# Multiplying a norm's factor into the products instead of their inputs, in a two-layer decoder step

## The chip, the core and the metric

The kernel runs on one core of a Trainium2 chip. Its time is the device time of one execution in microseconds (us); three runs of the kernel before took 3342.1, 3348.75 and 3351.01. PE is the matrix engine (TensorE), DVE the vector engine, ACT the scalar engine, POOL GpSimd; SP (SyncE) only issues transfers here, and ACT issues those of the weights.

## The reference

Two layers of a decoder process a prompt of 1024 tokens and 64 tokens of 8 sampled sequences, 1088 columns of 1024 features. Each layer is a mixer and a feed-forward, both behind a norm:

```python
def rmsnorm(x, g):
    return x * rsqrt(mean(x * x) + eps) * g

x = x + mixer(rmsnorm(x, norm_mix)) @ w_out
h = rmsnorm(x, norm_ffn)
x = x + (silu(h @ w_gate) * (h @ w_up)) @ w_down
```

The first layer's mixer is a short convolution on a product of two projections beside a linear recurrence (RWKV-7) over 8 heads. The second layer's is causal attention with forget gates over 8 heads, for the samples over 1024 cached rows each in paged memory as well, beside a state-space scan (SSD) in chunks of 128 tokens with its own causal convolution. The states, keys and values are outputs too. A last norm makes y.

## The kernel before

**Tiles.** Activations lie with features on the partitions, 8 tiles of 128 features by the columns of a half. There are two halves: H0 has the 64 sample columns and 512 of the prompt (576, handled in groups of 320 and 256), H1 the other 512. In layer 1's feed-forward the samples go with the second half instead: F0 has 512 columns and F1 576. A weight tile is 128 columns of a product for all 1024 inputs.

**Dense products.** Weights and activations are both split into a high and a low part, and each of the 8 feature tiles takes three matmuls (hh by wh, hl by wh, hh by wl; mm3, lines 204 to 206), all into one of four PSUM banks ("acc"). load_w (line 191) fetches a weight tile on ACT's queue, ACT rounds it to wh (line 196), and POOL, or DVE late in the kernel, takes the difference wl (line 198).

**The norms.** rms (line 227) squares eight tiles on ACT, adds them on DVE (line 239), sums over partitions with matmuls against ones on PE (line 245), takes the power on POOL (line 224) and broadcasts the factor over the partitions with matmuls (line 255). rms_split then makes x * g * r on DVE (line 269) and its two parts (lines 218, 219). These parts are what the next products read, so the next product begins after all of this. A call of rms_split makes 10 yields.

**The order of the work.** The functions are generators, and each yield ends a step. `weave(dense, side, rate)` emits the steps of a dense generator and, for each, `rate` steps of a side generator that does a mixer's small work. There are five weaves, with RATE = (5.5, 6, 1.8, 1.8, 1): the first two put the recurrences of H0 and H1 beside projections and H0's feed-forward; the third and fourth put `side`, which is latency(H0) and then latency(H1), beside third() (H1's layer-0 output and feed-forward, norm, and layer-1 projections) and beside F0's output product and feed-forward (ffn). These two are called with rest=False, and what is then left of the side comes from drain(side) (line 1570). latency(H0) has 32 steps of attention units, 25 of gates by token and scan, and 249 of the cached rows' attention (decode); latency(H1) has 32 attention units and 24 of the scan. F1's feed-forward comes last; its y (line 852) is read back from the buffers where attention and scan of H1 and the samples' decode leave it.

A scheduler orders each engine's instructions at build time by program order and a simulated readiness; the engines then run their queues in order, and wait on semaphores.

**The second half's attention** (line 1111) goes through 4 pairs of heads. For each pair the queries and keys (qa, qb, ka, kb, one buffer each) are loaded by SP. A unit is 128 queries of a head: scores into two PSUM banks ("fs", lines 1153 to 1155), mask and maximum on DVE (lines 1157 to 1161), exponentials on ACT (line 1164), reciprocal and scaling on DVE (lines 1167, 1168), transposes (line 1174), copies (line 1175), products with v (line 1182). The scan (line 1349) comes after it and writes y through ysp1.

Of the kernel before, what the change touches and what calls it, by code (L numbers as in the profile page):

```python
# [19 lines left out]
P = 128  # L20
D = 1024
# [21 lines left out]
CF = (3, 6)  # L43
# [27 lines left out]
# the second feed-forward takes the samples with the second half, since their attention is the last to be done  # L71
# [3 lines left out]
# columns of the parameter pack  # L75
# [9 lines left out]
# columns of the constant packs: 0 for both layers, 1 for the first mixer, 2 for the second, 3 for the cached rows  # L85
# [69 lines left out]
class K:  # L155
    """What the stages share: the builder, the pools and the constants on chip."""

    xp = None
    # PSUM banks: the dense products', the mixers' short-lived ones, their chains', and the ones with sums over many steps
# [26 lines left out]
    def parts(self, H):  # L186
        """Tiles for the two float32r parts of an activation of a half."""
        return [[self.bp.tile([P, H.W], F32R, name=n, tag="%s%d" % (n, H.i), bufs=KT) for _ in range(KT)] for n in ("hh", "hl")]


def load_w(k, src, n=D):
    nc = k.nc
    raw = k.wp.tile([P, D], F32, name="wraw", tag="wraw", bufs=2)[:, :n]
    nc.scalar.dma_start(raw, src)
# [27 lines left out]
def rsqrt(k, out, x):  # L222
    """x ** -0.5 of a few columns."""
# [3 lines left out]
def rms(k, H, xs, width, groups=None, ft=None, tag="acc"):  # L227
    """1 / sqrt(mean over features of x^2 + eps) on every partition: (columns, PSUM bank) per group."""
# [32 lines left out]
def rms_split(k, H, xs, gname):  # L261
    """rmsnorm(x) * g as two float32r parts."""
    nc = k.nc
    h = k.parts(H)
    rs = yield from rms(k, H, xs, D)
    for i in range(KT):
        v = k.ft(H)
        for a, b, r in rs:
            nc.vector.scalar_tensor_tensor(v[:, a:b], xs[i][:, a:b], k.col(gname, i), r, op0=ALU.mult, op1=ALU.mult)
        split(k, h[0][i], h[1][i], v, nc.gpsimd if i % 2 else nc.vector)  # L270
        if i % 2:
            yield
    return h
# [7 lines left out]
class Even:  # L281
    def __init__(self, k, pool):
# [9 lines left out]
        nc.gpsimd.memset(self.o_shift, 0.0)  # L292
        k.load_con(pool, 1)
        # the parts of the two small products' weights: the first part twice, for the two parts of what they take
# [12 lines left out]
        self.dv = pool.tile([P, 30], F32, name="dv")  # L307
        dv = self.dv
        nc.vector.tensor_scalar(dv[:, 0:14], k.pp[:, PP["mu"]:PP["mu"] + 14], -1.0, 1.0, op0=ALU.mult, op1=ALU.add)
        for o, n, f in ((14, "w0", 0.5), (18, "a0", 0.5), (22, "ka", 0.5), (26, "kk", -0.5)):  # L310
            nc.vector.tensor_scalar(dv[:, o:o + 4], k.pp[:, PP[n]:PP[n] + 4], f, None, op0=ALU.mult)
# [22 lines left out]
    def short_conv(self, H, h):  # L334
        k = self.k
        nc = k.nc
        for i in range(4):
# [4 lines left out]
            for a, b in H.groups:  # L342
                nc.scalar.copy(gcs[:, a:b], gemm_tile(k, wc, h, a, b))
# [23 lines left out]
            for a, b in H.groups:  # L367
                pb = gemm_tile(k, wb, h, a, b)
                nc.vector.tensor_mul(cv[:, a:b], cv[:, a:b], pb)
# [3 lines left out]
    def shift_mix(self, H, h, i, dp, ds):  # L373
        """Column tile i of the projection, mixed with the token before: z + mu * (before - z); dp prompt, ds samples."""
# [3 lines left out]
        w = load_w(k, k.A["wi0"][12 + i])  # L378
# [5 lines left out]
        for a, b in H.groups:  # L384
            acc = gemm_tile(k, w, h, a, b)
# [14 lines left out]
    def project(self, H, h):  # L400
# [1300 lines left out]
```

## Time and profile before

| what | value |
|---|---|
| runs | 3342.1, 3348.75, 3351.01 us; median 3348.75 |
| span of the profiled execution | 3342.5 us |
| PE busy | 3166.9 us, 95% |
| DVE busy | 1918.7 us, 57% |
| ACT busy | 1063.7 us, 32% |
| POOL busy | 843.0 us, 25% |

The profiled execution has the span as its own time; nothing else of it is shown, and the span lies between the lowest run and the median. PE is nearly always busy in the records. A busy PE is not PE at its peak: matmuls overlap, their ends are modelled, and a lower granted clock stretches them. So a stretch of the program is read with three numbers: its length, PE's busy time in it and the granted clock, 1.00 being the upper of its two levels.

### The profile page before, as it was taken

How to read it: one execution, taken by the hardware profiler on the slowest of the kernel's cores; microseconds unless marked ns; L12 is line 12 of the kernel's file. 1: busy time of each engine (PE TensorE's matmuls, PEld its weight loads, DVE VectorE, ACT ScalarE, POOL GpSimd, SP SyncE). 2: the span in 40 equal slices, each digit the busy share in tenths (PEclk: the TensorE clock that was granted, in tenths of full speed). 3: DMA queues.
4: the chain of work that ended last, by engine and by line, in shares of the span. 5: the costliest groups of instructions: out<-in, count | busy, mean ns of one | idle time of the engine just before them, and what ended most of it. 6: DMA issues, size and time to landing. Idle time of an engine off the chain costs nothing. (4 is left out here: it accounts for less than half of the span.)

```text
span 3342.5 us, 63321 instructions
## 1 busy us (share of the span) xinstructions
PE 3166.9 (95%) x25213; PEld 2667.2 (80%) x25213; DVE 1918.7 (57%) x3663; ACT 1063.7 (32%) x2083; POOL 843.0 (25%) x565
## 2 busy tenths in 40 slices
PE   7999999999999998999899999999999988999998
PEld 7887667777899998976677676766777767899998
DVE  6766646575544447656665457555646665554445
ACT  4333323333222223345322224232225543322222
POOL 3433233333233333301300102011010002333332
PEclk9999999999999998999899999999999999999999
DMA  5322233221122235543345557875553324232222
GB/s 178 116 66 82 87 99 114 65 65 57 51 72 83 82 112 160 178 151 124 98 155 171 192 161 228 240 233 158 164 177 118 123 89 151 69 104 82 83 82 79
DMA packets 238471, 409.20 MB, mean 122 GB/s; under 512 B 37632, under 2 KB 129664, under 8 KB 238176
## 3 DMA queue, kind: packets, MB, share of 16 engines
q10 hardware_dynamic: 63232, 218.80, 20.2%
q1 hardware_dynamic: 165584, 152.27, 15.2%
q0 software_dynamic: 9360, 34.08, 2.9%
q8 instruction: 199, 3.26, 0.4%
q14 instruction: 96, 0.79, 0.1%
HBM read 352.23 MB, written 52.81 MB: 121 GB/s over the span
## 5 line engine op out<-in xcount | busy, mean ns | idle before, releaser
L204 PE MATMUL acc<-hh,wh 128*128 128x320 f32 (+2 forms) x3720 | 1262.6, 341 | 14.0 <-ACT hh L218 10.7
L206 PE MATMUL acc<-hh,wl 128*128 128x320 f32 (+2 forms) x3720 | 1254.6, 337 | 7.2 <-POOL wl L198 6.4
L205 PE MATMUL acc<-hl,wh 128*128 128x320 f32 (+2 forms) x3720 | 1254.2, 338 | 7.1 <-DVE hl L219 5.1
L198 POOL TENSOR_TENSOR wl<-wraw,wh 128x1024 fp32r<-128x1024 f32 x229 | 549.2, 2399 | 988.3 <-ACT wh L196 931.2
L204 PEld LDWEIGHTS acc<-hh,wh 128*128 128x128 f32 x3720 | 711.2, 192 | 90.6 <-ACT hh L218 14.5
L196 ACT CAST wh<-wraw 128x1024 fp32r<-128x1024 f32 (+1 forms) x398 | 415.9, 1045 | 1145.5 <-PE acc L205 1021.9
L205 PEld LDWEIGHTS acc<-hl,wh 128*128 128x128 f32 x3720 | 712.3, 192 | 71.7 <-DVE hl L219 8.4
L206 PEld LDWEIGHTS acc<-hh,wl 128*128 128x128 f32 x3720 | 712.5, 192 | 70.9 <-POOL wl L198 8.1
L893 DVE TENSOR_TENSOR x<-x,acc 128x320 f32<-128x320 f32 (+2 forms) x528 | 270.6, 528 | 144.8 <-PE acc L206 143.0
L204 PE MATMUL acc<-hidh,wh 128*128 128x320 f32 (+2 forms) x1056 | 349.8, 337 | 3.7 <-ACT hidh L218 3.3
L205 PE MATMUL acc<-hidl,wh 128*128 128x320 f32 (+2 forms) x1056 | 353.2, 335 | 0.0
L206 PE MATMUL acc<-hidh,wl 128*128 128x320 f32 (+2 forms) x1056 | 350.2, 333 | 0.4 <-DVE wl L198 0.4
L198 DVE TENSOR_TENSOR wl<-wraw,wh 128x1024 fp32r<-128x1024 f32 x169 | 205.5, 1217 | 116.5 <-ACT wh L196 96.1
L1297 POOL DMA_INDIRECT kv<-in_cv,vidx x64 | 75.1, 1173 | 630.4 <-DMA kv<-in_ck 363.8
L204 PEld LDWEIGHTS acc<-hidh,wh 128*128 128x128 f32 x1056 | 198.8, 189 | 28.0 <-ACT hidh L218 6.0
L205 PEld LDWEIGHTS acc<-hidl,wh 128*128 128x128 f32 x1056 | 200.1, 190 | 17.5 <-issue 1.4
L206 PEld LDWEIGHTS acc<-hidh,wl 128*128 128x128 f32 x1056 | 200.3, 190 | 16.2 <-issue 0.9
L219 DVE TENSOR_TENSOR hidl<-ft,hidh 128x512 fp32r<-128x512 f32 (+2 forms) x148 | 178.6, 1207 | 57.1 <-ACT hidh L218 55.8
L881 DVE SCALAR_TENSOR_TENSOR ft<-ft,acc 128x320 f32<-128x320 f32 (+2 forms) x132 | 70.1, 531 | 221.4 <-PE acc L206 218.0
L875 DVE SCALAR_TENSOR_TENSOR ft<-ft,acc 128x320 f32<-128x320 f32 (+2 forms) x132 | 69.7, 528 | 190.2 <-ACT ft L874 190.1
L218 ACT CAST hidh<-ft 128x512 fp32r<-128x512 f32 (+2 forms) x148 | 75.1, 507 | 120.4 <-DVE ft L881 117.2
L1249 DVE STREAM_TRANSPOSE kt<-kv 128x1024 f32<-128x1024 f32 x64 | 79.3, 1240 | 35.8 <-DMA kv<-in_ck 21.1
(340 smaller groups left out, 3360.1 us busy)
## 6 DMA issues: line engine op xcount, KB each, us to landing
wraw<-in_wi ACTq DMA_DIRECT2D x100, 512.0 KB
wraw<-in_wg ACTq DMA_DIRECT2D x88, 512.0 KB
wraw<-in_wu ACTq DMA_DIRECT2D x88, 512.0 KB
wraw<-in_wd ACTq DMA_DIRECT2D x88, 512.0 KB
kv<-in_ck SPq DMA_DIRECT2D x512, 64.0 KB
wraw<-in_wo ACTq DMA_DIRECT2D x32, 512.0 KB
ka<-kp SPq DMA_DIRECT2D x48, 128.0 KB
x<-in_xT SPq DMA_DIRECT2D x16, 288.0 KB
```

What stands on the lines that cost most here:

```text
L196: nc.scalar.copy(wh, raw)
L198: k.low.tensor_sub(wl, raw, wh)
L204: mm(acc, wh, xh, start=first, stop=False)
L205: mm(acc, wh, xl, start=False, stop=False)
L206: mm(acc, wl, xh, start=False, stop=last)
L218: k.nc.scalar.copy(hh, v)
L219: (eng or k.nc.vector).tensor_sub(hl, v, hh)
L875: nc.vector.scalar_tensor_tensor(s[:, a:b], s[:, a:b], 1.0, pc, op0=ALU.add, op1=ALU.mult)
L881: nc.vector.scalar_tensor_tensor(s[:, a:b], s[:, a:b], 0.5, pu, op0=ALU.mult, op1=ALU.mult)
L893: nc.vector.tensor_add(xs[n][:, a:b], xs[n][:, a:b], acc[:, :b - a])
L1249: V.transpose(kt, kr)
L1297: nc.gpsimd.indirect_dma_start(out=v, out_offset=None, in_=A["cv"].rearrange("o (s r) c -> (o s) (r c)", r=2), in_offset=bass.IndirectOffs ...
```

## The change

A class Norm takes the place of rms_split. The parts that the products read are made of x * g, without the factor. The sum of squares is kept as the tiles of x are made or arrive. The ones-products, the power, and the broadcast are emitted inside the first product that uses the parts, after its sixth and sixteenth feature tile (third and eighth for a half in one group). The factor, r, goes to SBUF, and each product is multiplied by it on DVE as it leaves PSUM. In the feed-forward the gate's product is multiplied by r for the tanh, and by r again, which covers the factor of the product with w_up.

The first weight tile and the next are fetched before x. In the first layer the recurrence's constants are loaded after three products, H1's norm comes right after, and the second half's short convolution goes ahead of H0's output product instead of beside norms. The weaves keep their rates; the norm's yields are gone. The scan writes its G in L and a decayed state in place; zp has one buffer; the ten first steps of F1, not twenty, stand beside the last of F0's.

```diff
+class Norm:
...
+        self.due = (6, 16) if len(H.groups) > 1 else (3, 8)
...
+    def square(self, x):
+        k = self.k
+        if self.ss is None:
+            self.ss = k.bp.tile([P, self.H.W], F32, name="rn", tag="rn%d" % self.H.i, bufs=1)
+            k.nc.scalar.activation(self.ss, x, AF.Square)
+            return
+        sq = k.ft(self.H)
+        k.nc.scalar.activation(sq, x, AF.Square)
+        k.nc.vector.tensor_add(self.ss, self.ss, sq)
+
+    def part(self, i, x):
+        if not i:
+            self.hl = self.k.parts(self.H)
+        k, g = self.k, self.k.col(self.gname, i)
+        k.nc.scalar.mul(self.hl[0][i], x, g)
+        k.nc.vector.scalar_tensor_tensor(self.hl[1][i], x, g, self.hl[0][i], op0=ALU.mult, op1=ALU.subtract)
+
+    def step(self):
...
+        if self.seen == self.due[0]:
+            pt = k.bank()
+            for j, (l, _, _) in enumerate(H.blocks):
+                nc.tensor.matmul(pt[:, j:j + 1], self.ss[:, l:l + P], k.con("ones"), start=True, stop=True)
+            self.rs = k.bp.tile([P, 16], F32, name="rs", tag="rs", bufs=2)
+            nc.vector.tensor_scalar(self.rs[:, 8:8 + nb], pt[:, :nb], 1.0 / D, EPS, op0=ALU.mult, op1=ALU.add)
+            rsqrt(k, self.rs[:, 0:nb], self.rs[:, 8:8 + nb])
+        elif self.seen == self.due[1]:
...
+                    nc.tensor.transpose(pb[:, c - o:c - o + P], self.rs[:, j:j + 1].to_broadcast([P, P]), k.con("ident"))
...
+                nc.scalar.copy(r[:, o:e], pb[:, 0:e - o])
+            self.r = r
...
@@ gemm_tile
+        if isinstance(h, Norm):
+            h.step()
...
@@ out_ffn
         xs.append(x)
-        yield
-    h = yield from beside(rms_split(k, H, xs, "nf%d" % l), fill)
+        nr.square(x)
+        if n < KT - 1:
+            yield
+    w = load_w(k, A["wg%d" % l][0])
+    for i, x in enumerate(xs):
+        nr.part(i, x)
+    yield
...
             s = k.ft(H)
+            t = k.ft(H)
             for (a, b), pc in zip(H.groups, pg):
-                nc.scalar.activation(s[:, a:b], pc, AF.Tanh, scale=0.5)
-                nc.vector.scalar_tensor_tensor(s[:, a:b], s[:, a:b], 1.0, pc, op0=ALU.add, op1=ALU.mult)
+                nc.vector.tensor_mul(t[:, a:b], pc, nr.r[:, a:b])
+                nc.scalar.activation(s[:, a:b], t[:, a:b], AF.Tanh, scale=0.5)
+            nc.vector.tensor_mul(t, t, nr.r)
+            nc.vector.scalar_tensor_tensor(s, s, 1.0, t, op0=ALU.add, op1=ALU.mult)
...
@@ Odd.dense
-                    nc.scalar.mul(t[:, a:b], gemm_tile(k, w, h, a, b), f)
+                    nc.vector.scalar_tensor_tensor(t[:, a:b], gemm_tile(k, w, h, a, b), f, h.r[:, a:b], op0=ALU.mult, op1=ALU.mult)
...
@@ ssd
-                    g_ = tl([P, 128], "G", 3)
-                    V.scalar_tensor_tensor(g_[:n, :n], L[:n, :n], tok[:n, c, 64 + hd:65 + hd], gt[:n, c, g, :n], op0=ALU.mult, op1=ALU.mult)
+                    V.scalar_tensor_tensor(L[:n, :n], L[:n, :n], tok[:n, c, 64 + hd:65 + hd], gt[:n, c, g, :n], op0=ALU.mult, op1=ALU.mult)
...
@@ hybrid_step
-        x0 = x_in(H0)
         k.pp = cp.tile([P, NPP], F32, name="pp")
         nc.sync.dma_start(k.pp, A["pp"])
+        w0 = load_w(k, A["wi0"][24])
         k.load_con(cp, 0)
+        k.ahead = [fetch(k, A["wi0"][16])]
+        h0 = norm_in(H0)
...
             def third():
-                x1 = yield from ffn0(H1)
-                h = yield from rms_split(k, H1, x1, "nm1")
+                h = yield from ffn0(H1)
                 yield from m.dense(H1, h)
...
-            weave(ffn, islice(ffn1, 20), RATE[4])
+            weave(ffn, islice(ffn1, 10), RATE[4])
```

PE in the second half's attention, in the kernel before: scores (L1155), transposes (L1174) and products with v (L1182) of two units, between them F0's dense matmuls (L204 to 206; hidh and hidl are the parts of the feed-forward's hidden tile).

```order
L206 MATMUL acc<-hh,wl 128x512
L204 MATMUL acc<-hidh,wh 128x512
L205 MATMUL acc<-hidl,wh 128x512
L206 MATMUL acc<-hidh,wl 128x512
L204 MATMUL acc<-hidh,wh 128x512
L1182 MATMUL rk<-pT,vt 64x128 x10
L1155 MATMUL fs<-ka,qa 128x512
L1155 MATMUL fs<-kb,qb 128x512
L1155 MATMUL fs<-ka,qa 128x256
L1155 MATMUL fs<-kb,qb 128x256
L204 MATMUL acc<-hidh,wh 128x512
L1174 MATMUL rk<-con_222,s 128x128 x6
```

The same attention in the changed kernel, where scores are L1233, transposes L1252 and products with v L1260.

```order
L1233 MATMUL fs<-ka,qa 128x512
L1233 MATMUL fs<-kb,qb 128x512
L1233 MATMUL fs<-ka,qa 128x384
L1233 MATMUL fs<-kb,qb 128x384
L1252 MATMUL rk<-con_212,s 128x128 x7
L1233 MATMUL fs<-ka,qa 128x512
L1233 MATMUL fs<-kb,qb 128x512
L1233 MATMUL fs<-ka,qa 128x512
L1233 MATMUL fs<-kb,qb 128x512
L1252 MATMUL rk<-con_212,s 128x128 x7
L1233 MATMUL fs<-ka,qa 128x512
L1233 MATMUL fs<-kb,qb 128x512
```

The dense matmuls that stood between the units stand ahead of them now. In the whole queue, 28 of the 32 units and the scan of H1 come after F0's last dense matmul, with 48 dense matmuls of F1's beside them.

PE at the norm of F1's feed-forward, in the kernel before: the ones-products (L245) and the broadcast (L255) between the last of w_out's products and the first of w_gate's (128x320).

```order
L205 MATMUL acc<-hl,wh 128x256
L206 MATMUL acc<-hh,wl 128x256
L245 MATMUL acc<-con_222,ft 128x1 x5
L255 MATMUL acc<-con_222,rs 128x64
L255 MATMUL acc<-con_222,rs 128x128 x4
L204 MATMUL acc<-hh,wh 128x320
L204 MATMUL acc<-hh,wh 128x256
L205 MATMUL acc<-hl,wh 128x320
```

There in the changed kernel, inside the first product of w_gate: L210 to 212 are mm3, L310 the ones-products, and the transposes that broadcast the factor come some 25 matmuls later.

```order
L212 MATMUL acc<-hh,wl 128x256
L210 MATMUL acc<-hh,wh 128x256
L310 MATMUL rk<-con_212,rn 128x1 x5
L211 MATMUL acc<-hl,wh 128x256
L212 MATMUL acc<-hh,wl 128x256
L210 MATMUL acc<-hh,wh 128x256
```

No dense matmul stands behind the broadcast any more, but for the emptying of its bank.

## Rows read from the trace of the kernel before

**Rows 1.** The page's part 1: busy us, share of the span, instructions of each engine.

```profile
PE 3166.9 (95%) x25213; PEld 2667.2 (80%) x25213; DVE 1918.7 (57%) x3663; ACT 1063.7 (32%) x2083; POOL 843.0 (25%) x565
```

**Rows 2.** Windows round five norms: from:to length, busy (instructions) per engine, clock, DMA.

```profile
640.00:700.00 60.00, 55.57 (x655) 41.36 (x652) 41.33 (x94) 19.40 (x44) 22.03 (x18) 0.91 0.19 60
1250.00:1272.00 22.00, 15.75 (x86) 12.94 (x85) 17.66 (x34) 7.51 (x11) 12.12 (x10) 0.77 0.37 121
1506.00:1520.00 14.00, 10.16 (x49) 8.40 (x45) 9.10 (x20) 5.66 (x14) 3.93 (x3) 0.66 0.31 96
2274.00:2292.00 18.00, 13.77 (x80) 8.22 (x79) 8.09 (x14) 3.17 (x6) 5.97 (x5) 0.62 0.58 167
2883.00:2903.00 20.00, 12.68 (x61) 11.35 (x61) 12.47 (x23) 6.69 (x10) 7.77 (x5) 0.66 0.10 34
```

**Rows 3.** PE's waits, 2883 to 2903: total, times, longest, in us.

```profile
PE acc L245 <- DVE ft L239: 4.1, 1, 4.1
```

**Rows 4.** Windows, the woven stretch at the end of layer 1's mixer.

```profile
2500.00:2700.00 200.00, 199.77 (x1257) 159.52 (x1258) 130.05 (x296) 103.50 (x248) 0.00 (x0) 1.00 0.36 113
2700.00:2812.00 112.00, 98.23 (x498) 75.61 (x497) 64.95 (x142) 40.10 (x84) 18.80 (x12) 0.91 0.36 118
2812.00:2840.00 28.00, 23.06 (x115) 19.54 (x115) 14.80 (x20) 10.21 (x14) 7.37 (x5) 0.94 0.64 205
```

**Rows 5.** Timeline of the start: start, length in us, engine, line, tiles [idle before].

```profile
5.30 0.68 ACT L237 ACTIVATE ft<-x 128x576 f32<-128x576 f32 x1 [2.35 <-DMA x<-in_xT]
...
18.49 2.29 PE L245 MATMUL acc<-con,ft 128*128 128x1 f32 x10 [18.49 <-DVE ft L239]
...
26.13 0.85 PE L204 MATMUL acc<-hh,wh 128*128 128x320 f32 x2 [1.34 <-ACT hh L218]
```

**Rows 6.** Timeline, two units of the second half's attention, 2571 to 2581.

```profile
2571.05 0.50 PE L1155 MATMUL fs<-ka,qa 128*128 128x512 f32 x1
...
2573.97 0.69 ACT L1164 ACTIVATE s<-fs,nm 128x512 f32<-128x512 f32 x1 [0.29 <-DVE nm L1161]
...
2575.17 0.39 PE L1155 MATMUL fs<-ka,qa 128*128 128x512 f32 x1
...
2575.81 0.19 PEld L204 LDWEIGHTS acc<-hidh,wh 128*128 128x128 f32 x1
...
2577.42 0.77 PEld L1174 LDWEIGHTS rk<-con,s 128*128 128x128 f32 x6
...
2578.88 1.53 PE L1182 MATMUL rk<-pT,vt 128*64 128x128 f32 x24
...
2580.34 0.50 PE L1155 MATMUL fs<-ka,qa 128*128 128x512 f32 x1
```

**Rows 7.** Timeline of SP's DMA issues at a change of head pair.

```profile
2557.70 1.09 SPq L1135 DMA_DIRECT2D ka<-kp  x2
```

**Rows 8.** ACT's lines, 2500 to 2700: busy us, mean ns, idle before.

```profile
L1164 ACT ACTIVATE s<-fs,nm 128x512 f32<-128x512 f32 x64 | 38.6, 612 | 17.2 <-DVE nm L1161 15.4 <-DMA ka<-kp 1.6
L1175 ACT COPY pT<-rk 128x512 f32<-128x512 f32 (+3 forms) x62 | 28.3, 506 | 34.3 <-PE rk L1174 31.8 <-DVE fs L1157 2.2
...
L1164 ACT ACTIVATION_READ_ACCUMULATOR s<-fs,nm 128x1 f32 x64 | 13.2, 206 | 0.0
```

**Rows 9.** The chain that ended last, 2695 to 2830: start, us, what.

```profile
2703.52 2.51 DMA yb<-yo
2706.98 6.92 DMA bc<-xc
...
2800.96 4.70 DMA yb<-y
...
2812.35 6.02 DMA ft<-yb
```

**Rows 10.** DVE's lines, 2700 to 2812.

```profile
L198 DVE TENSOR_TENSOR wl<-wraw,wh 128x1024 fp32r<-128x1024 f32 x7 | 8.5, 1215 | 9.1 <-ACT gt L1376 9.1
L893 DVE TENSOR_TENSOR x<-x,acc 128x512 f32<-128x512 f32 x12 | 8.1, 684 | 6.1 <-PE acc L206 6.0
```

More of the change, by code (lines that the diff above doesn't have):

```diff
@@ L41 @@
 VY = 3
-CF = (3, 6)
+CF = 3
 class Half:
@@ L158 @@
     xp = None
+    ahead = ()
     PS = {"acc": 4, "rk": 2, "ch": 2, "fs": 2}
@@ L258, in rms, with __init__, __getitem__ @@
     return out
[L261 to L271, printed above, removed]
-            yield
-    return h
+class Norm:
+    def __init__(self, k, H, gname):
+        self.k, self.H, self.gname = k, H, gname
+        self.ss = self.r = None
+        self.seen = 0
+        self.due = (6, 16) if len(H.groups) > 1 else (3, 8)
+    def __getitem__(self, i):
+        return self.hl[i]
+    def square(self, x):
[14 more added lines that the diff above has]
+    def step(self):
+        if self.r is not None:
+            return
+        self.seen += 1
+        k, H = self.k, self.H
+        nc = k.nc
+        nb = len(H.blocks)
+        if self.seen == self.due[0]:
[6 more added lines that the diff above has]
+        elif self.seen == self.due[1]:
+            r = self.ss
+            for lo in range(0, nb, 4):
+                bs = list(enumerate(H.blocks))[::-1][lo:lo + 4][::-1]
+                pb = k.bank()
+                o = bs[0][1][1]
+                for j, (_, c, w) in bs:
+                    nc.tensor.transpose(pb[:, c - o:c - o + P], self.rs[:, j:j + 1].to_broadcast([P, P]), k.con("ident"))
+                e = bs[-1][1][1] + bs[-1][1][2]
+                nc.scalar.copy(r[:, o:e], pb[:, 0:e - o])
+            self.r = r
@@ L292, in __init__, with ready @@
         nc.gpsimd.memset(self.o_shift, 0.0)
+        self.dv = pool.tile([P, 30], F32, name="dv")
+        dv = self.dv
+        nc.vector.tensor_scalar(dv[:, 0:14], k.pp[:, PP["mu"]:PP["mu"] + 14], -1.0, 1.0, op0=ALU.mult, op1=ALU.add)
+        for o, n, f in ((14, "w0", 0.5), (18, "a0", 0.5), (22, "ka", 0.5), (26, "kk", -0.5)):
+            nc.vector.tensor_scalar(dv[:, o:o + 4], k.pp[:, PP[n]:PP[n] + 4], f, None, op0=ALU.mult)
+    def ready(self):
+        k, pool = self.k, self.mp
+        nc, A = k.nc, k.A
         k.load_con(pool, 1)
@@ L840, in finish, with out_ffn @@
             nc.sync.dma_start(k.ysp0[self.H.i][4 + i][:, self.ts], oo[:, sl])
-def out_ffn(k, H, l, fill=iter(()), last=None):
+def out_ffn(k, H, l, nxt=None, last=None):
     nc, A = k.nc, k.A
@@ L908, in out_ffn @@
                     drain(down([(q, w)], a, b))
+                if nxt and g == NF // GH - 1:
+                    for x in xs[4 * q:4 * q + 4]:
+                        nxt.square(x)
                 yield
@@ L1496, in hybrid_step, with norm_in, ffn0 @@
         scratch(k, dp)
-        def x_in(H):
-            xs = [k.xt(H) for _ in range(KT)]
-            for i in range(KT):
-                nc.sync.dma_start(xs[i], A["xT"][i][:, H.cols()])
-            return xs
-        x0 = x_in(H0)
         k.pp = cp.tile([P, NPP], F32, name="pp")
         nc.sync.dma_start(k.pp, A["pp"])
+        w0 = load_w(k, A["wi0"][24])
         k.load_con(cp, 0)
-        def ffn0(H, fill=iter(())):
-            xs = yield from out_ffn(k, H, 0, fill)
+        k.ahead = [fetch(k, A["wi0"][16])]
+        def norm_in(H):
+            h = Norm(k, H, "nm0")
             for i in range(KT):
+                x = k.xt(H)
+                nc.sync.dma_start(x, A["xT"][i][:, H.cols()])
+                h.square(x)
+                h.part(i, x)
+            return h
+        h0 = norm_in(H0)
+        def ffn0(H):
+            h = Norm(k, H, "nm1")
+            xs = yield from out_ffn(k, H, 0, h)
+            for i in range(KT):
+                h.part(i, xs[i])
                 nc.sync.dma_start(k.xs[H.i][i], xs[i])
-            return xs
+            return h
         def final(H, xs, groups=None):
@@ L1526, in hybrid_step @@
         with tc.tile_pool(name="m0", bufs=1) as mp, tc.tile_pool(name="mps", bufs=1, space=PSUM) as k.mps:
-            norm = rms_split(k, H0, x0, "nm0")
-            next(norm)
             m = Even(k, mp)
-            h0 = drain(norm)
-            h1 = []
+            proj = m.project(H0, h0, w0)
+            for _ in islice(proj, 3):
+                pass
+            m.ready()
+            h1 = norm_in(H1)
+            drain(proj)
+            conv1 = m.short_conv(H1, h1)
+            out = []
             def first():
@@ L1535, in first @@
                 yield from m.project(H1, h1)
-                yield from islice(conv1, CF[0])
-            def norm1():
-                h1.extend((yield from rms_split(k, H1, x_in(H1), "nm0")))
-            weave(m.project(H0, h0), norm1(), 1)
-            x0 = []
-            conv1 = m.short_conv(H1, h1)
+                yield from islice(conv1, CF)
             def second():
-                x0.extend((yield from ffn0(H0, islice(conv1, CF[1]))))
+                yield from conv1
+                out.append((yield from ffn0(H0)))
             weave(first(), m.recurrence(H0), RATE[0])
             weave(second(), m.recurrence(H1), RATE[1])
-            h0 = drain(beside(rms_split(k, H0, x0, "nm1"), conv1))
-            drain(conv1)
             m.finish()
```

70 lines of the change are left out of this document (39 added, 31 removed).

## The prediction

> **What bounds the kernel now.** I read the page's busy shares first: PE is busy for 3166.9 of the span's 3342.5 us, DVE for 57% of it [rows 1]. So the sum of matmuls is the floor, and a change that leaves the matmuls as they are can only give back idle time of PE and stretches of reduced clock, 176 us of idle in all, or add to them. Next I cut the span into stretches by stage [rows 2]: each row shows the stretch's length, PE's busy time in it, and the granted clock. Around the norms PE falls idle for 4 to 8 us and the clock averages 0.62 to 0.91 of its upper level, 2.4 GHz; a mean between 0.5 and 1 is a mixture of that level and 1.2 GHz. Who is waited for is told by PE's waits [rows 3]: at the second half's last norm PE's ones-products wait 4.1 us for the running sum of squares (L239), and the factors' broadcast stands behind the power on POOL. Last I read the woven stretch near the end, 2500 to 2840 us, where the attention and the scan of the second half run beside dense products: PE is busy 199.77 of 200 us in its first part [rows 4]. Nothing waits there because there is always a dense matmul to go on with.
>
> The profile's span is 3342.5 us and one of the three runs took 3342.1, so nothing measurable lies around the span; the median, 3348.75, is 6.25 above. I make the sum on the span and add 6.25 at the end.
>
> **What the change removes: PE's stops at the norms.** Products are taken of x times g, and r multiplies them afterwards, so no product waits for the sum, the power and the broadcast, except where its own bank is emptied. Idle time plus the clock's part, each from its row in [rows 2], as (length - busy) + (1 - clock) x busy:
> - 640 to 700: 4.43 + 5.0 = 9.4, I take 6.
> - 1250 to 1272: 6.25 + 3.6 = 9.9, I take 7.
> - 1506 to 1520: 3.84 + 3.5 = 7.3, I take 6.
> - 2274 to 2292: 4.23 + 5.2 = 9.5; part of it is cached rows' loads, which stay. I take 6.
> - 2883 to 2903: 7.32 + 4.3 = 11.6, I take 10. Its wait of 4.1 [rows 3] goes entirely.
>
> Two smaller stretches like these, about 520 (the wait for y, which conv1's products now fill) and 2040, I put at 4 and 3. That is 42, and 47.7 for the five shown if they vanish whole, some 55 with the two.
>
> The start: PE's first instruction begins at 18.49 and its first dense product at 26.13, while x's first tile is squared at 5.30 [rows 5]. With the weights fetched ahead and the parts made tile by tile, the first product could begin near 10. But ACT now has a square and a multiply per tile, 2 x 0.68 at that row's price, so eight tiles take 11 us, and on POOL the power for r is queued behind the wl of two weights. In ACT's new order the second half's parts also stand ahead of a weight's DMA, so a later weight comes late. I take 8, bounds 0 and 16 (26.13 - 10). Sum of gains: 50, bounds 25 (half of it) and 71.
>
> **What it adds.** DVE gets the multiplications by r. A 512-wide one costs 0.68 (the residual's addition, [rows 10]); a gate product gets two more, 4 x 22 of them, one with PSUM and one without: some 110 us; the projections, q, k, v, z, gates and convolutions get about one each, 90 products, some 65, partly in place of ACT's; the norms' own stt go, 64 x 0.8 = 51. Net about +125 us on DVE, which goes from 57% to 61% of the span [rows 1]. PE's four accumulating banks cover it except where DVE is nearly full; I take 5, bounds 0 and 20. The scan's tile L in place of G, the single zp buffer and the ten early steps of the last feed-forward in place of twenty I put at nothing: the scan's 32 products are chained through other tiles anyway, and zp's writer is DVE itself, in order; if that cover is gone each is within those 20.
>
> **What it moves: the weave.** This is where I expect the time to be decided. Side steps are emitted at 1.8 for each dense step in third() and F0, and those weaves end with the dense steps (rest=False); whatever is left of the side goes out by drain(side) with nothing dense beside it. A step is a yield, so I count yields. Before, out_ffn has 2 for y, 8 for w_out, 10 for the norm (rms 4 + 1 + 1, rms_split 4) and 66 for the feed-forward: 86. After, 2 + 7 + 1 + 66 = 76: the norm's steps are gone although they held hardly any PE work. third() is 86 + 10 + 25 = 121 before and 76 + 25 = 101 after; with F0's 86 and 76, 207 and 177 dense steps. Times 1.8 that releases 372 side steps before and 318 after. The side needs 306 for the first half (gates by token, scan, cached rows) and 56 for the second (32 units of attention and 24 of the scan): 362. Before, all of it fits in the weave. After, 318 - 306 = 12 of the last 56 do, and 44 come after F0's last dense step. The order of PE says the same: before, dense products stand between the units of the second half's attention; after, 28 of the 32 units and the entire scan have 48 dense matmuls beside them. More of the last output product and feed-forward, F1, cannot begin in the meantime: the 48 are the first four feature tiles into four banks, 12 as each pair's y arrives, and the rest of y is that scan's output.
>
> So what PE's order loses is a stretch bound by its chain, not by PE. Its length:
> - Attention, 28 units. A unit's scores go to two PSUM banks (there are two), DVE adds the mask and takes the maxima, ACT takes the exponentials, and only then are the banks free for the next. From one unit's first score to the next's it took 4.1 us and then 5.2 with dense matmuls between [rows 6]. The first bank's exponential had ended at 2573.97 + 0.69 = 2574.66, so 0.5 of the 4.1 was the queue of dense matmuls ahead of the score at 2575.17: without them 3.6, and a little less for the narrow units; I take 3.5. Lower bound: ACT, the engine with most work per unit, (38.6 + 28.3 + 13.2) / 32 = 2.5 [rows 8]. Upper: 5.2. So 98, bounds 70 and 146.
> - Three changes of head pair. The pair's 26 loads go through SP's queue at about 0.55 us an issue (1.09 for 2, [rows 7]); the queries' and keys' tiles have one buffer, so the first head's 13 must issue after the last use: 7 each, 21, bounds 0 and 40.
> - From the attention's last output to the scan's first product: the output's store 2.5 and the load of B and C 6.9 [rows 9]: 9, which before lay beside dense products.
> - The scan: it runs from the end of that load, 2713.90, to y's store at 2800.96 [rows 9], 87 us, woven. DVE is busy for 64.95 of the 112 us around it [rows 4], of which dense steps' wl and residual additions are 8.5 and 8.1 [rows 10] and smaller ones about 8, so 40 are its own. Between 40 and 87 I take 60, nearer to DVE's.
> - y's store 4.7 and its load 6.0 [rows 9], and the first split: 12, as before.
> Together 200, bounds 131 and 294. PE's own work in it: a unit has 0.64 for scores (2575.17 to 2575.81), 0.77 for the transposes and half of 1.53 for the product with v, 2.1 [rows 6], so 59; the scan about 30 (half of the 498 matmuls there are its own, most of them a quarter as wide as the dense ones: a third of the 98.23, [rows 4], is an estimate); the 48 dense, narrower than a half's, some 6: 95. PE thus idles for 105. What the trace of before loses in the same work is (200 - 199.77) + (112 - 98.23) + (28 - 23.06) = 19, and by the clock (0.91 and 0.94) 11 more: 30 [rows 4]. The loss is 75, bounds 6 and 169.
>
> The sum: 3342.5 - 50 + 5 + 75 = 3372.5, and with 6.25 for the median 3379, rounded to 3380.
>
> The Trainium skill (Perfetto Trace Analysis, section Optimization Strategy) says that a kernel whose most-contended engine changes over time may gain by interleaving such regimes; here the change does the reverse, and the trace agrees in that PE is at 199.77 of 200 us where they are interleaved.
>
> **Rivals.**
> 1. The chain is no slower than its busiest engine (not slower, the other side). If two units overlap fully, ACT at 2.5 a unit gives 70, the scan goes at DVE's 40, pair changes hide behind the units, and 12 remain for y: 122; PE's 95 leaves 27 idle, about the 30 of before. The loss is gone and the time is 3342.5 - 50 + 5 - 3 + 6.25 = 3301. It decides from the point where the whole stretch is under 170 us: there the loss of PE's time falls below the net gain of 45. Against it stand two banks and 4.1 us a unit [rows 6], for it that ACT and DVE are both well under 70% busy there [rows 4]. The Trainium skill (Perfetto Trace Analysis, section Identifying the Most-Contended Engine) makes the engine of highest occupancy the bound; by that rule the stretch would go as in this rival, and the unit times in the trace speak against it.
> 2. Halfway: 3.0 a unit and a scan of 50 with the pair changes half hidden give 84 + 10 + 9 + 50 + 12 = 165, a loss of 40, and 3342.5 - 50 + 5 + 40 + 6.25 = 3344: no change.
> 3. The stretch is as slow as before's pace or slower: with PE half idle its clock may fall, as it does around the norms [rows 2], to 1.2 GHz; then PE's 2.1 a unit doubles in the chain for the parts that aren't overlapped, say 1 a unit, and the stretch is 228, or 275 at 5.2 a unit and 87 for the scan: 3407 to 3454.
> 4. The change doesn't remove the stops: the ones-products, which need all eight squares, sit in the first product on PE's in-order queue, so PE stops there instead of before it. Then the gain is half, 25, and the time 3404.
>
> **How the numbers follow.** A measurement of this kernel tells about 0.3%, 10 us, from no change: 3339 to 3359. The likeliest case, 3380 with a range of its own from 3360 to 3402, has 0.45; the slower stretch (3407 to 3454) 0.14, the half gain (3404) 0.10, the halfway case (3344) 0.16, and the fast chain with what lies around it (3301 to 3338) 0.15. So faster 0.15, within 0.3% 0.16, slower 0.69. The range that holds it 8 times in 10 runs from 3330 to 3432: it cuts off the lower part of rival 1 and the upper part of rival 3, a tenth each.
>
> **What would show it.** In the profile of the changed kernel: no wait of PE for the running sum before the last feed-forward's first product, and no drop of clock there; the first dense product near 10 us; a stretch of about 200 us ahead of the last feed-forward in which PE is busy about half of it, scores 3.5 us apart; idle PE ended by DVE's maxima, ACT's exponentials and transposes. Wrong would be: that stretch under 170 us, or PE over 70% busy in it; then the time is at or below the one before. Were scores 3.5 us apart and the total still lower, the norms would have given back more than I read from their rows.

## The result, and the profile after

The changed kernel takes 3453.22 us (median of four, 3449.43 to 3461.24) against 3349.88 in the runs beside it: a ratio of 1.0308, 95% interval 1.0288 to 1.0327. It is slower, as forecast, but by 103 us where 31 were forecast, and outside the range that ended at 3432.

The profile's span is 3447.7 us, 105.2 longer than before; its own run took 3449.43, so 1.7 us do lie around a span. The page's part 1 and the row of granted clock (40 slices, tenths of the upper level) are, for the changed kernel:

```profile
PE 3197.9 (93%) x25177; PEld 2691.4 (78%) x25177; DVE 2177.8 (63%) x3927; ACT 1047.3 (30%) x2015; POOL 802.9 (23%) x529
...
PEclk9999999999999999999999999999999877899999
```

Against [rows 1] PE is busy 31 us longer, though it does the same dense matmuls, and the clock's row shows where: slices 32 to 35, from 2672 to 3017 us. DVE has 259 us more. The attention's stretch by windows (length, busy and instructions of PE, PEld, DVE, ACT, POOL, then clock, DMA share, GB/s):

```profile
2600.00:2665.00 65.00, 64.48 (x346) 47.97 (x338) 34.57 (x45) 14.62 (x18) 7.88 (x6) 1.00 0.44 148
2690.00:2735.00 45.00, 30.21 (x200) 23.16 (x198) 21.21 (x52) 18.75 (x51) 2.34 (x1) 0.83 0.30 93
2735.00:2782.00 47.00, 33.24 (x208) 26.15 (x208) 19.94 (x57) 19.18 (x55) 0.00 (x0) 0.79 0.23 69
2782.00:2830.00 48.00, 33.20 (x208) 26.19 (x208) 20.04 (x58) 20.13 (x56) 0.00 (x0) 0.78 0.24 69
2830.00:2871.00 41.00, 29.78 (x187) 24.24 (x187) 16.54 (x46) 16.60 (x47) 0.00 (x0) 0.72 0.01 2
2871.00:2942.00 71.00, 44.48 (x225) 34.31 (x226) 40.55 (x110) 26.04 (x65) 11.52 (x9) 0.74 0.26 86
...
2686.80:2942.00 255.20, 172.57 (x1036) 135.57 (x1037) 120.67 (x326) 101.67 (x273) 14.90 (x11) 0.77 0.22 68
```

The second, third and fourth pair of heads begin with these scores:

```profile
2719.74 0.50 PE L1233 MATMUL fs<-ka,qa 128*128 128x512 f32 x1 [1.41 <-ACT s L1242]
...
2767.61 0.50 PE L1233 MATMUL fs<-ka,qa 128*128 128x512 f32 x1 [1.41 <-ACT s L1242]
...
2815.41 0.50 PE L1233 MATMUL fs<-ka,qa 128*128 128x512 f32 x1 [1.41 <-ACT s L1242]
```

Up to 2665 PE is full, as in [rows 4]; then it is busy for 63 to 73% of the windows at a mean clock of 0.72 to 0.83. The pairs begin 48 us apart: 6.0 us a unit, pair change included. Above 2871 it is the scan. From the end of F0's last dense matmuls, 2686.8, to the end of the scan, 2942, PE is busy 172.6 of 255 us at a clock of 0.77: 83 us idle and 40 more by the clock.

The norms did change as meant. The windows after layer 0's first feed-forward and around the last norm read:

```profile
1272.00:1294.00 22.00, 18.83 (x139) 17.49 (x138) 18.85 (x23) 8.23 (x12) 10.03 (x5) 1.00 0.44 120
2950.00:3010.00 60.00, 58.91 (x418) 58.05 (x418) 32.30 (x39) 23.00 (x33) 21.83 (x10) 0.95 0.35 115
```

Against 0.77 and 0.66 in [rows 2] the clock stays at 1.00 and 0.95 (F1's first 6 us; from 2956 on it is 1.00), and PE idles 3.2 of 22 us and 1.1 of 60. PE's waits in the second window and just ahead of it:

```profile
PE acc L210 <- ACT hh L226: 6.7, 1, 6.7
PE rk L321 <- POOL rs L232: 0.9, 1, 0.9
```

The 4.1 us for the running sum [rows 3] are gone; what is left is one wait of 6.7 for F1's y, which before fell into 2812 to 2840, and 0.9 for the power. The first dense product starts at 8.43 instead of 26.13 [rows 5]:

```profile
8.43 0.85 PE L210 MATMUL acc<-hh,wh 128*128 128x320 f32 x2 [8.43 <-ACT hh L297]
```

A table of how far the n-th dense matmul is behind that of before, from the two traces, tells where time went. The feed-forwards' and the norms' places are fixed points in it; where side work is spread otherwise (7200 to 10800) it only says how dense the weave is:

| dense matmul | before, us | after, us behind |
|---|---|---|
| 0 | 26.1 | -17.7 |
| 400 | 90.5 | -1.6 |
| 2400 | 750.1 | 7.8 |
| 3600 | 999.7 | 25.3 |
| 5200 | 1213.7 | 26.0 |
| 5600 | 1291.8 | 7.5 |
| 10400 | 2671.5 | -81.4 |
| 11200 | 2903.8 | 100.7 |
| 14327 | 3327.4 | 105.0 |

So there are three things to explain: the 93 us between 5600 and 11200 (of the 182 between 10400 and 11200, 81 only give back what the thinner weave had run ahead), the start's 17.7 of which 1.6 is left at 90 us, and 27 lost from there to 3600, in the first layer's weaves.

### The profile page after: what moved, and what is told of

The parts are those of the page before. It is cut to its first block, busy times and chain, and to the rows that moved or that the text cites. A ratio compares the mean times of both kernels' runs of the same rounds, so it can differ in the third digit from the quotient of the medians.

```text
span 3447.7 us, 63382 instructions
## 1 busy us (share of the span) xinstructions
PE 3197.9 (93%) x25177; PEld 2691.4 (78%) x25177; DVE 2177.8 (63%) x3927; ACT 1047.3 (30%) x2015; POOL 802.9 (23%) x529
## 5 line engine op out<-in xcount | busy, mean ns | idle before, releaser
L210 PE MATMUL acc<-hh,wh 128*128 128x320 f32 (+2 forms) x3720 | 1268.1, 342 | 26.2 <-ACT hh L226 10.0
L212 PE MATMUL acc<-hh,wl 128*128 128x320 f32 (+2 forms) x3720 | 1258.9, 339 | 20.7 <-POOL wl L204 16.6
L210 PEld LDWEIGHTS acc<-hh,wh 128*128 128x128 f32 x3720 | 714.8, 193 | 112.4 <-issue 18.6
L204 POOL TENSOR_TENSOR wl<-wraw,wh 128x1024 fp32r<-128x1024 f32 x225 | 543.2, 2415 | 1083.9 <-ACT wh L202 999.5
L210 PE MATMUL acc<-hidh,wh 128*128 128x320 f32 (+2 forms) x1056 | 348.2, 337 | 1.5 <-ACT hidh L226 1.4
L945 DVE TENSOR_TENSOR ft<-acc,rn 128x256 f32<-128x256 f32 (+2 forms) x132 | 70.1, 533 | 264.8 <-PE acc L212 257.4
L204 DVE TENSOR_TENSOR wl<-wraw,wh 128x1024 fp32r<-128x1024 f32 x173 | 210.9, 1219 | 27.4 <-ACT wh L202 22.6
L210 PEld LDWEIGHTS acc<-hidh,wh 128*128 128x128 f32 x1056 | 198.5, 189 | 25.8 <-ACT hidh L226 4.9
L947 DVE TENSOR_TENSOR ft<-ft,rn 128x576 f32<-128x576 f32 (+1 forms) x88 | 148.4, 1686 | 37.0 <-ACT ft L946 37.0
L954 DVE SCALAR_TENSOR_TENSOR ft<-ft,acc 128x320 f32<-128x320 f32 (+2 forms) x132 | 70.1, 531 | 106.8 <-PE acc L212 102.6
```

Source lines behind the costliest of these rows:

```text
L204: k.low.tensor_sub(wl, raw, wh)
L210: mm(acc, wh, xh, start=first, stop=False)
L212: mm(acc, wl, xh, start=False, stop=last)
L945: nc.vector.tensor_mul(t[:, a:b], pc, nr.r[:, a:b])
L947: nc.vector.tensor_mul(t, t, nr.r)
L954: nc.vector.scalar_tensor_tensor(s[:, a:b], s[:, a:b], 0.5, pu, op0=ALU.mult, op1=ALU.mult)
```

## The experiments

**1. The steps put back.** The changed kernel, with empty steps where the norms had theirs:

```diff
         nr.part(i, x)
     yield
+    for _ in range(10 if H.i else 0):
+        yield
...
                 h = yield from ffn0(H1)
+                for _ in range(10):
+                    yield
```

> The changed kernel with ten empty steps put back where the norm of F0 and of H1's feed-forward and of third() had them, so that the two late weaves release as many side steps as before; nothing else. If the loss is the side's last 44 steps standing alone (the weave theory), the stretch before the last feed-forward is woven again and some 98 of the 104 us come back: 3345 to 3365. If the loss is DVE's added work (2178 us busy instead of 1919) or the waits it makes, the time stays within 20 us of the changed kernel's: 3433 to 3473.

Measured: 3356.58 us, ratio to before 1.0018 (1.0003 to 1.0033). Of the 103 us 97 are back, by 30 yields that hold no instruction: 10 each for H1's and F0's feed-forward and for third(). Its windows:

```profile
2500.00:2700.00 200.00, 198.48 (x1215) 155.41 (x1214) 129.26 (x271) 90.37 (x206) 0.00 (x0) 1.00 0.42 127
2700.00:2812.00 112.00, 98.24 (x560) 75.39 (x559) 73.74 (x176) 51.07 (x120) 10.29 (x8) 0.93 0.24 81
```

PE is full again, 198.48 of 200, with the attention woven as in [rows 4].

**2. The rate raised.** The changed kernel with `RATE = (5.5, 6, 2.1, 2.1, 1)` in place of 1.8.

> The changed kernel with 2.1 instead of 1.8 side steps for each dense step in the third and fourth weave, nothing else: 177 x 2.1 = 372, the number released before. Weave theory: as with the ten steps put back, 3345 to 3370. DVE theory: 3433 or more, since the side's DVE work then comes denser.

Measured: 3354.95, ratio 1.0017 (1.0000 to 1.0033). The same, by another way to the same count.

**3. The old kernel with too few steps.** Before, with `RATE = (5.5, 6, 1.54, 1.54, 1)`; its norms are untouched.

> The kernel before with 1.54 instead of 1.8 side steps in the third and fourth weave, norms as they were: 207 x 1.54 = 319, the number that the changed kernel releases. Weave theory: it loses what the changed kernel lost there, 3430 to 3455. If the loss needs the new norms or DVE's added work: within 20 us of before, 3335 to 3370.

Measured: 3447.03, ratio 1.0304 (1.0279 to 1.0330). Nearly the changed kernel's whole loss, without a line of its norms. Windows over the same pairs of heads:

```profile
2690.00:2735.00 45.00, 32.86 (x206) 25.68 (x206) 21.00 (x57) 20.65 (x55) 2.36 (x1) 0.78 0.31 90
2735.00:2782.00 47.00, 32.62 (x216) 25.78 (x212) 20.49 (x58) 20.22 (x55) 0.00 (x0) 0.79 0.25 75
2782.00:2830.00 48.00, 33.32 (x213) 26.29 (x209) 20.20 (x58) 19.71 (x55) 0.00 (x0) 0.78 0.23 63
```

PE's busy time is the changed kernel's within 3 us, and the clock within 0.05.

**4. PE kept busy in the stretch.** The changed kernel, with matmuls on a constant tile after each step that stands alone:

```diff
-            drain(side)
...
+            for _ in side:
+                dummy = k.bank("acc")
+                for i in range(8):
+                    nc.tensor.matmul(dummy, filler[:, 0:128], filler, start=i == 0, stop=i == 7)
```

> The changed kernel with eight matmuls of 512 columns on a constant tile after each of the 44 side steps that stand alone (their result is read by nobody): 1.84 us of PE work a step at the upper clock. If the lower clock lengthens the attention's chain (5.5 us a unit, granted clock 0.78), the clock returns to the upper level and a unit takes 4 to 5 us in spite of the added work: 20 to 40 us less than the changed kernel. If the chain's waits on DVE and ACT set the pace and the clock does not matter, a unit takes 5.5 us or up to 1.8 more, and the time is 3450 to 3500.

Measured: 3434.28 (two runs, 3429.14 and 3439.41), ratio to before 1.0262 (1.0227 to 1.0297): 19 us faster than the changed kernel, just short of the expected 20, and on two runs that lie 10 apart. Windows, the last one in the scan:

```profile
2735.00:2782.00 47.00, 47.00 (x312) 37.03 (x311) 21.98 (x63) 21.77 (x62) 0.00 (x0) 1.00 0.31 91
2782.00:2830.00 48.00, 47.98 (x316) 37.69 (x316) 23.26 (x67) 21.63 (x60) 0.00 (x0) 1.00 0.26 78
...
2875.00:2940.00 65.00, 40.48 (x234) 31.69 (x233) 40.99 (x108) 20.21 (x50) 9.28 (x7) 0.78 0.24 76
```

In the attention the clock is at 1.00, PE is full, and a pair of heads takes 42 us from first score to first score instead of 48: 5.3 a unit, above the expected 4 to 5. The traces confirm the gain there: from the third unit's first score to the attention's last output it takes 165.9 us (2693.3 to 2859.2) instead of 186.4 (2684.2 to 2870.6). The lower clock is thus a part of the slow pace, at least 0.7 us of the 6.0, since the added matmuls stand in the same queue. PE did some 84 us of added work (360 matmuls in the trace, 0.23 from start to start) and finished earlier. The last of them ends at 2872.7, though: the scheduler put those of the scan's steps into the attention as well. The scan ran without them at a clock of 0.78, and what the clock costs there was not measured.

**5. The second half's norm later.** From here on with the rates of experiment 2.

```diff
             m.ready()
+            drain(proj)
             h1 = norm_in(H1)
-            drain(proj)
```

> The changed kernel with the 2.1 rates, and the second half's norm (load, squares, parts) emitted after the first half's projection instead of after its third product. In the profile the 17.7 us that the start gains are gone by 90 us, with a weight's issue on ACT's queue at 33.60 behind the second half's parts and 5.9 us of PE waiting for wl. If that queue eats the gain: some 8 us of it last past 100 us and, if the recurrence's chain does not take them back, the time is 3343 to 3350. If the recurrence's chain sets the time in any case: 3351 to 3360, as with the rates alone.

Measured: 3340.32, ratio to before 0.9977 (0.9958 to 0.9995), 14.6 below the rates alone (13 by the ratios, since the two were not timed side by side) and below both expected ranges. In the changed kernel's trace, PE's waits from 28 to 100 us and ACT's queue (casts and weight issues) read:

```profile
PE acc L212 <- POOL wl L204: 6.1, 3, 3.7
PE rk L602 <- DMA la<-zl: 3.9, 1, 3.9
```

```profile
15.06 0.34 ACTq L194 DMA_DIRECT2D wraw<-in_wi  x1
...
33.67 0.33 ACTq L194 DMA_DIRECT2D wraw<-in_wi  x1
...
41.79 1.03 ACT L202 CAST wh<-wraw 128x1024 fp32r<-128x1024 f32 x1
```

Between two issues of weights 18.6 us pass; a square and five of the second half's parts stand between them on ACT. With the norm later the issues stand at

```profile
14.59 0.35 ACTq L194 DMA_DIRECT2D wraw<-in_wi  x1
...
23.65 0.34 ACTq L194 DMA_DIRECT2D wraw<-in_wi  x1
...
29.51 0.33 ACTq L194 DMA_DIRECT2D wraw<-in_wi  x1
```

and PE's largest wait from 20 to 100 us is

```profile
PE acc L212 <- POOL wl L204: 1.0, 1, 1.0
```

At dense matmul 400 this kernel is 18.2 us ahead of before, where the rates alone are 2.3 ahead.

**6. One multiplication left out.** The gate's second multiplication by r; the product with w_up then lacks the norm's factor.

```diff
-            nc.vector.tensor_mul(t, t, nr.r)
-            nc.vector.scalar_tensor_tensor(s, s, 1.0, t, op0=ALU.add, op1=ALU.mult)
+                nc.vector.scalar_tensor_tensor(s[:, a:b], s[:, a:b], 1.0, pc, op0=ALU.add, op1=ALU.mult)
```

> The changed kernel with the 2.1 rates, without the second multiplication by r of the gate's product (the factor of the product with w_up is left out): the sum takes its operand from PSUM as before. This takes 148 us of DVE's busy time away, 118 of it in 44 multiplications that stand 2.7 us each while POOL makes wl. If DVE's added work in the first layer's weaves is why the norms' gains are lost there (29 us behind before at dense matmul 3600): 15 to 25 us faster than the rates alone, 3330 to 3340. If it is covered: 3351 to 3360.

Measured: 3331.67, ratio 0.9947 (0.9929 to 0.9966), 23 below the rates alone. DVE is busy 2034.6 us instead of 2173.5, and at dense matmul 3600 the kernel is 10.5 us behind before instead of 28.9. What that multiplication costs is seen by form in the changed kernel's lines (busy, mean ns, idle before):

```profile
L947 DVE TENSOR_TENSOR ft<-ft,rn 128x576 f32<-128x576 f32 x44 | 118.4, 2692 | 35.2 <-ACT ft L946 35.2
...
L945 DVE TENSOR_TENSOR ft<-acc,rn 128x512 f32<-128x512 f32 x44 | 30.4, 691 | 123.6 <-PE acc L212 121.1 <-ACT rn L323 2.4
...
L947 DVE TENSOR_TENSOR ft<-ft,rn 128x512 f32<-128x512 f32 x44 | 30.0, 681 | 1.8 <-ACT ft L946 1.8
```

With 512 columns it takes 681 ns, with 576 columns 2692. The 576-wide ones are those of halves whose wl is made on POOL. At one place of the timeline:

```profile
758.60 2.36 POOL L204 TENSOR_TENSOR wl<-wraw,wh 128x1024 fp32r<-128x1024 f32 x1 [2.69 <-ACT wh L202]
...
758.87 2.70 DVE L947 TENSOR_TENSOR ft<-ft,rn 128x576 f32<-128x576 f32 x1 [0.60 <-ACT ft L946]
...
761.89 0.74 DVE L948 SCALAR_TENSOR_TENSOR ft<-ft 128x576 f32<-128x576 f32 x1
```

DVE's multiplication of two SBUF tiles starts 0.27 us after POOL's subtraction and lasts 2.70, to 0.6 after POOL's end; a like instruction beside it takes 0.74. Of the 44, the 42 that overlap a POOL instruction take 2.8 at the median, the other two 0.75; each of the 42 ends 0.61 us after the POOL instruction that it overlaps. In the kernel before, line 875's sum with one operand in PSUM (128x256) overlaps a POOL instruction in 41 of 44 cases and takes 0.42 at the median, 0.41 in the other three.

**7. More steps in the second weave.** `RATE = (5.5, 7, 2.1, 2.1, 1)`.

> The changed kernel with the 2.1 rates, and 7 instead of 6 side steps for each dense step in the second weave. If the second half's recurrence ends late there because its steps are emitted too thinly (at dense matmul 3320 instead of 3198): it ends by 3200 and the time is 10 to 20 us less, 3335 to 3345. If the recurrence's chain runs as fast as it can: 3350 to 3365.

Measured: 3352.56, ratio 1.0016 (1.0000 to 1.0033): no change. Too few steps for the recurrence are not what costs the time.

**8. r squared in the product with w_up.** Experiment 5 with this, for H0's feed-forward in layer 0 alone:

```diff
+                    nc.vector.scalar_tensor_tensor(s[:, a:b], s[:, a:b], 1.0, pc, op0=ALU.add, op1=ALU.mult)
...
+                r2 = k.m0.tile([P, 576], F32, name="r2")
+                nc.vector.tensor_mul(r2, nr.r, nr.r)
...
+                    nc.vector.scalar_tensor_tensor(t[:, a:b], pu, 0.5, r2[:, a:b], op0=ALU.mult, op1=ALU.mult)
+                    nc.vector.tensor_mul(s[:, a:b], s[:, a:b], t[:, a:b])
```

> The changed kernel with the 2.1 rates, the second half's norm after the first half's projection, and, in the first layer's feed-forward of the first half only, r squared multiplying the product with w_up as it leaves PSUM instead of r multiplying the gate's product a second time in SBUF (one small state tile moves into a hidden tile's buffer to make room). Nothing is left out. If DVE's multiplications that stand behind POOL's wl are what the first layer loses: it gets back about half to all of the 18 us that leaving the factor out gave there, 3322 to 3333. If DVE's added instructions as such are the cost, whichever operand they read: 3336 to 3345, as with the two other edits alone.

Measured: 3336.71, ratio 0.9963 (0.9950 to 0.9975), 3.6 below experiment 5. By its total this falls into the second range, 3336 to 3345, not into the one for POOL's wl, 3322 to 3333. At dense matmul 3600, however, it is 0.5 us ahead of before and experiment 5's kernel 20.2 behind, so the first layer's gain is there; at the end of the profile the two differ by 4 the other way. The two were therefore timed again side by side.

> The same kernel as n_late, timed again on one chip beside n_up: 3338 to 3343 if it stands where it stood.

> The same kernel as n_up, timed again on one chip beside n_late. In the profile it was 20 us ahead of n_late when the first layer's weaves ended, and 4 us behind at the end, while the medians had it 3.6 us ahead. If the first layer's gain lasts: 10 us or more below n_late5. If the second layer's weave takes it back: within 5 us of n_late5.

Measured: 3346.90 (ratio 0.9989, 0.9972 to 1.0005) and 3336.26 (0.9961, 0.9943 to 0.9978), 10.6 apart. Experiment 5's kernel did not stand where it stood: it is above its expected 3343, and 9 us below the rates alone by the ratios where it was 13. With 20.7 us between the two kernels at dense matmul 3600 and 3.6 and 10.6 between their medians, a part of the gain lasts; how much of it the second layer takes back is not settled, since executions of one kernel differ by 10 us and more. The lines of the multiplication that reads two SBUF tiles are now

```profile
L962 DVE TENSOR_TENSOR ft<-ft 128x320 f32<-128x320 f32 x22 | 10.8, 489 | 0.6
...
L962 DVE TENSOR_TENSOR ft<-ft 128x256 f32<-128x256 f32 x22 | 9.3, 424 | 0.6
```

489 and 424 ns: they come right after the reads of PSUM, before POOL's next wl, and only the split behind them waits for POOL, as it did before. This is the fastest full version of the kernel that was run, 12.7 us below before. Not all of the first layer's loss is explained by it: it is 18.2 us ahead of before at dense matmul 400 and 0.5 at 3600 (18.5 and 0.2 in the second profile). What takes these 18 us in the recurrences' weaves stays open; experiment 7 speaks against too few steps.

## Why the prediction was wrong

Between the forecast, 3380, and the 3453 measured lie 73 us. The weave's loss makes 22 of them, 97 instead of 75. The other 51 are the net gain of norms, start and DVE's work: 45 were forecast, and without the weave's loss the kernel is 6 slower than before.

**The direction and its mechanism were right.** The yields were counted correctly, 318 side steps for 362 (experiment 4's trace has one more standing alone than the 44), and the last units stand alone. Three experiments turn this on and off by the count alone: 97 and 98 us back in the changed kernel, 97 lost in the old one. The rival that a chain without dense work runs at its busiest engine's pace fell; by [rows 8] ACT's 2.5 us a unit were expected there, and 6.0 were taken. The Trainium skill (Perfetto Trace Analysis, section Identifying the Most-Contended Engine) takes the engine of highest occupancy for the bottleneck. In this stretch that is PE, with 33.2 of 47 us in one window, and no engine's busy time gives the 6.0. The Trainium skill's advice to interleave (Perfetto Trace Analysis, section Optimization Strategy) holds here: woven, the same side steps cost 97 us less (experiments 1 to 3).

**That the time lies in rival 3's range is in part luck.** The clock did fall, as that rival has it. But its upper end, 3454, was made of 5.2 us a unit and 87 for the scan, where 6.0 and 71 with the hand-over were measured, and of the net gain of 45, which was not there.

**The step on the unit's pace failed.** The prediction took 3.5 us, from the shorter of two distances between scores in [rows 6]. Over the stretch the units take 3.5 to 9.5 and on average 6.0. In the kernel before, from first score at 2500.0 to last at 2689.6, 32 units took 190 us: 5.9 to 6.1 each, woven. Taking the dense work away did not make the units faster, but the clock fell with it, from 1.00 to 0.78; at 1.00, beside experiment 4's matmuls, they take 5.3. Two rows out of 32 units were taken for the pace of all. One of the longer cycles in the changed kernel (timeline, PE and ACT and DVE), and the clock in its last part:

```profile
2745.64 0.50 PE L1233 MATMUL fs<-ka,qa 128*128 128x512 f32 x1 [1.41 <-ACT s L1242]
...
2747.29 0.61 DVE L1246 TENSOR_SCALAR s<-s,nm 128x768 f32<-128x768 f32 x1
...
2748.04 1.51 PE L1252 MATMUL rk<-con,s 128*128 128x128 f32 x6 [1.30 <-DVE s L1246]
...
2749.17 0.86 ACT L1253 COPY pT<-rk 128x512 f32<-128x512 f32 x2 [3.12 <-PE rk L1252]
...
2749.80 2.83 PE L1260 MATMUL rk<-pT,vt 128*64 128x128 f32 x24 [0.25 <-ACT pT L1253]
...
2751.05 0.22 ACT L1242 ACTIVATION_READ_ACCUMULATOR s<-fs,nm 128x1 f32 x1
...
2752.56 0.80 PE L1233 MATMUL fs<-ka,qa 128*128 128x512 f32 x1
```

```profile
2748.00:2752.60 4.60, 4.31 (x31) 3.61 (x31) 1.53 (x5) 2.10 (x6) 0.00 (x0) 0.50 0.01 4
```

From the scores at 2745.64 the chain goes on to the scaling of the unit before, its transposes, their copy, and the product with v, and only behind this, in PE's queue, to the next scores at 2752.56. ACT had finished the exponentials at 2751.27, so the banks were free 1.3 us earlier: in this cycle the queue decides, not the banks. In the next one the scores wait for the exponentials. Over the attention, 2686.8 to 2871, PE's 56 idle us are mostly these two waits, the transposes for the scaling and the scores for their banks:

```profile
PE rk L1252 <- DVE s L1246: 18.1, 12, 3.3
PE fs L1233 <- ACT s L1242: 17.9, 13, 1.8
```

The product with v takes 2.83 here against 1.53 in [rows 6], and the six transposes 1.51 against 0.81 in the same place of the kernel before: the clock is at 0.50 here and was at 1.00 there.

```profile
2577.61 0.81 PE L1174 MATMUL rk<-con,s 128*128 128x128 f32 x6
```

The attention part measured 184 us (2686.8 to 2871) where 98 + 21 were forecast. The scan with its hand-over measured 71 where 9 + 60 were: as a sum that term was right. The upper bound, 5.2 a unit, was from the same two rows and too low as well. With y the stretch measured 263 us (to F1's first product at 2949.64) where 200 were forecast. PE's own work of 95 was sized too low too: 172.6 busy us at a clock of 0.77 are some 133 at the upper level. So in the prediction's own terms the loss is 263 - 133 - 30 = 100, near the 97 of the experiments: the stretch was forecast 63 us too short and PE's work 38. The two errors partly cancelled.

**The step on the clock was put in a rival and belonged in the sum.** The clock fell to 0.72 to 0.83 in the stretch. Experiment 4 prices it for the attention, net of the work it adds: a unit at 5.3 instead of 6.0, some 20 us in all, which is a lower bound. For the scan it is not shown.

**The step on the net gain failed: the gains were there and were lost elsewhere.** With the weave repaired the change is worth +5 to +6 us (experiments 1 and 2) where -45 was forecast. The two norms outside the mixers' weaves gave more than was written down: in experiment 2, 17 us between dense matmuls 5200 and 5600 where 7 were taken, 12 between 10800 and 11200 where 10 were. What the norms inside the weaves gave cannot be read off. The start gave 17.7 and kept 2.3 of it in experiment 2: the stall behind the second half's parts was foreseen ("a later weight comes late") and priced at half; it took nearly all, 8 to 15 us by experiment 5 and its repetition.

**The step on DVE's cost failed.** It was 5 us with a bound of 20; the multiplication at 0.68 us each was read from a row whose other operand comes from PSUM [rows 10]. The added work is 259 us, not 125, and 118 of it is one line with both operands in SBUF, waiting for POOL. The trace of before had a row with such a pair, the split of the narrower group:

```profile
L219 DVE TENSOR_TENSOR hidl<-ft,hidh 128x256 fp32r<-128x256 f32 x44 | 107.2, 2435 | 16.7 <-ACT hidh L218 16.7
```

It took 2.4 us for 256 columns, three and more times the price that was taken for 512, and each of the 44 ends 0.28 us after the POOL instruction that it overlaps. Where PE has a chain to wait for DVE, in the recurrence's weaves, this shows in the time: leaving the line out gave 23 us (experiment 6). In F1, where DVE is covered, the same line costs nothing: from dense matmul 11600 to the end the distance stays at 103.9 to 105.0. The Trainium skill (SBUF — State Buffer, section Summary: rules for kernel authors) says that a DVE instruction with two SBUF inputs and a GpSimd instruction that reads SBUF exclude each other for an instruction's whole length. The trace agrees: 2.8 against 0.75 us, and DVE's end always 0.61 after POOL's.

**The convolution's zone** was part of those 5 us. It reads after, and before:

```profile
1370.00:1450.00 80.00, 70.57 (x520) 68.99 (x519) 73.37 (x135) 18.29 (x25) 23.80 (x10) 1.00 0.34 108
```

```profile
1362.00:1440.00 78.00, 75.08 (x561) 73.89 (x559) 60.93 (x112) 26.48 (x54) 24.06 (x10) 1.00 0.42 138
```

DVE went from 60.93 of 78 to 73.37 of 80 us, and PE from 2.9 idle to 9.4, all of it behind wl, whose cast stands behind an ACT instruction that waits for DVE. That was not tried by itself. With the edits of experiments 5 and 8 the change is worth -12 to -13 us; where the rest of the forecast 45 went is shown only in part, by this zone and by the 18 us in the first layer's weaves.

Two slips of the text above the result: the samples' cached rows are 2048 for each, not 1024, and the profiled run does take 1.7 us more than its span.

## What to carry to other kernels

Where a generator's steps are the currency that releases other work, count the yields before and after an edit: removing steps that hold nothing removes the work that was emitted on their account. Size a stretch that will stand alone by its mean pace over all its units, never by the best pair of rows. Price an added vector instruction from a row with the same operands in the same memories, and ask what GpSimd does at that moment.

## What was not expected of the hardware

The attention's chain took 48 us for 8 units alone and 46 to 50 woven with dense matmuls on the same PE, so the dense work beside it cost no time; the granted clock was 0.78 alone and 1.00 woven. 360 matmuls that nobody reads, 84 us of PE's time, made a kernel 19 us faster (two runs); the granted clock went from 0.78 to 1.00 beside them. A multiplication of two SBUF tiles took 0.75 us alone and 2.8 beside POOL's subtraction, ending 0.61 us after it in all 42 cases; a sum with one operand in PSUM took 0.42 beside POOL and 0.41 alone.
